# A drain between two users of one PSUM bank gives way to a one-column copy by ScalarE

## The chip, the cores and the metric

The kernel runs on one core of a Trainium2 chip. A core has five engines with a queue of their own: TensorE (PE in the profile, with its weight loads shown apart as PEld), VectorE (DVE), ScalarE (ACT), GpSimd (POOL) and SyncE (SP), which here only issues transfers. Every queue runs in the order in which it was filled, and engines wait for each other through semaphores. PE writes its products to PSUM, which has eight banks of 512 float32 columns on 128 partitions. The metric is the device time of one launch in microseconds.

## The reference, cut to what matters

The reference is a small latent diffusion trunk: two layers over 1024 latent tokens and 256 context tokens of width 1024, in float32. Layer 0 mixes tokens by differential attention, layer 1 by a state-space scan; each is followed by a squared-ReLU MLP. The change touches only the attention of layer 0:

```python
def attend(q, k, v):
    s = jnp.einsum('bqhcd,bkhcd->bhcqk', q, k).astype(jnp.float32)
    p = jax.nn.softmax(s, axis=-1)
    w = p[:, :, 0] - lam * p[:, :, 1]
    o = jnp.einsum('bhqk,bkhe->bqhe', w.astype(v.dtype), v)
    return rmsnorm(o, subln_g) * (1.0 - lambda_init)
```

There are eight heads. Each has two sets of queries and keys of width 64 (the index c), and one set of values of width 128. Latent queries read all 1280 keys, context queries the 256 context keys alone.

## The kernel before, in words

Float32 matmuls are made of three faster ones: every operand is split into a high and a low part, and high·high, high·low and low·high are added up in PSUM (`mm3`, L130 to L134; `split`, L136, whose high part is a copy by ACT at L137 and whose low part is a subtraction at L138).

**Attention (`phase_b`, L623)** goes through 72 units, nine for each head h. Unit u = 0 takes the 256 context queries, and each of the units u = 1 to 8 takes 128 latent queries. The profile shows them between about 224 and 903 us. In a unit the following happens:

- `scores` (L507) puts the scores of both sets into PSUM: set c = 0 in columns 0 to 1279, c = 1 in columns 1280 to 2559. The two sets use different halves of PE's rows (partitions 0 to 63 and 64 to 127), so a matmul of one set and a matmul of the other run at the same time. For u > 0 there are 21 matmuls in three groups of three rounds each: first c = 0 into bank 2 beside c = 1 into bank 3; then c = 0 into bank 0 beside c = 1 into bank 4; last c = 0 into bank 1 beside two short ones of c = 1, into banks 3 and 2. Bank 2 thus has two users: c = 0 in the first group, c = 1 in the third. Line 524 puts a drain of PE between the first and the second group.
- `maxima` (L529): DVE copies the scores of each set from PSUM to SBUF and takes their extremum on the way (L539).
- `exps` (L541): ACT takes exponentials and their sums (L549). `combine` (L552) makes p0 − lambda·p1 on DVE (L557 to L560).
- The transposes of the unit before (`w_part`, L562) and the copies that bring them to SBUF as high and low parts (`w_evac`, L577: L580 and L585 by ACT, L581 by DVE, L586 and L587 by POOL).
- Every second unit, the product with the values (`values`, L654) for a pair of units, and its copy out (`pair_out`, L665).
- Projections of the queries and keys of the next head (`proj_group`, L441), between the transposes.
- In five units out of nine, from head 1 on, `norm_pair` (L696) scales a pair of outputs of an older head: DVE multiplies (L697), ACT copies the high part (L137, tile `W<-W`), POOL subtracts the low part, and SP stores both. It is the last thing that such a unit gives to ACT. The condition in the loop (`n - 6 >= 9 and (n - 6) % 9 < 5`) makes it happen in the units u = 6, 7, 8 and in u = 0, 1 of the next head.

The order on PE, DVE, ACT and POOL in this phase is the order in which the loop is written (`manual`, L589); SP's transfers are placed by the scheduler. Dependencies are kept by the framework: two users of one PSUM bank are ordered by a semaphore whenever they are on different engines, and need none when both are on PE. After this phase the scheduler sets the order of all engines.

Of the kernel before, what the change touches and what calls it, by code (L numbers as in the profile page):

```python
# [9 lines left out]
AF = mybir.ActivationFunctionType  # L10
# [37 lines left out]
def shaped(ap, dims):  # L48
    if len(dims) == 1:
        return ap  # L50
    names = "abcd"[: len(dims)]
    kw = {n: d for n, d in zip(names[1:], dims[1:])}
    return ap.rearrange(f"p ({' '.join(names)}) -> p {' '.join(names)}", **kw)
# [17 lines left out]
class Prog:  # L71
# [410 lines left out]
    def lam_setup(self):  # L482
        nc, I = self.nc, self.I
        t, pr = self.fv(0, 256), self.fv(1, 2, 64)
        self.dma(t, I["attn_lambda"].rearrange("o a b -> o (a b)").to_broadcast((128, 256)))
        t4 = shaped(t, (2, 2, 64))
        nc.vector.tensor_tensor(pr, t4[:, :, 0], t4[:, :, 1], ALU.mult)
        st = self.lamc = self.cst.tile([128, 12], F32, name="lamc")
        nc.vector.tensor_reduce(st[:, 0:2], pr, AX.X, ALU.add)
        nc.scalar.activation(st[:, 2:4], st[:, 0:2], AF.Exp)  # L490
        nc.scalar.activation(st[:, 4:6], st[:, 2:4], AF.Ln)
        nc.vector.tensor_tensor(st[:, 4:6], st[:, 0:2], st[:, 4:6], ALU.subtract)
        nc.vector.tensor_scalar(st[:, 4:6], st[:, 4:6], 1.0, None, ALU.add)
        nc.vector.tensor_tensor(st[:, 2:4], st[:, 2:4], st[:, 4:6], ALU.mult)
        nc.vector.tensor_tensor(st[:, 6:7], st[:, 3:4], st[:, 2:3], ALU.subtract)
        nc.vector.tensor_scalar(st[:, 6:7], st[:, 6:7], -0.2, None, ALU.add)
        self.neglam = st[:, 6:7]
        self.dma(st[:, 7:8], I["attn_subln"].rearrange("o e -> e o"))
        nc.vector.tensor_scalar(st[:, 7:8], st[:, 7:8], 0.8, None, ALU.mult)
        self.sg = st[:, 7:8]  # L500
        self.ones = st[:, 8:9]
        nc.vector.memset(self.ones, 1.0)


# [2 lines left out]
    def scores(self, u, Q, K):  # L507
        mm = self.nc.tensor.matmul

        def tiles(qs, *parts):  # L510
            for n, (i, j) in enumerate(self.TERMS):
                for c, k0, k1, o in parts:
                    rows = slice(64 * c, 64 * c + 64)
                    mm(self.PS[:, o : o + k1 - k0], Q[rows, i, qs], K[j][rows, k0:k1], start=n == 0, stop=n == 2)  # L514

        if u == 0:
            for t in range(2):
                tiles(slice(128 * t, 128 * t + 128), (0, 0, 256, 512 * t), (1, 0, 256, 1024 + 512 * t))
            return
        qs = slice(128 * ((u - 1) % 2), 128 * ((u - 1) % 2) + 128)  # L520
        part = lambda c, k0, k1: (c, k0, k1, 1280 * c + k0)
        tiles(qs, part(0, 1024, 1280), part(1, 256, 512))

        self.nc.tensor.drain()
        tiles(qs, part(0, 0, 512), part(1, 768, 1280))
        tiles(qs, part(0, 512, 1024), part(1, 512, 768), part(1, 0, 256))

# [1690 lines left out]
```

## Time and profile before

| | |
|---|---|
| median of 3 runs | 2986.89 us (2981.88 to 2988.55) |
| the profiled execution's own time | 2989.72 us |
| its span, first to last instruction | 2987.9 us |
| mean granted clock of PE | 0.977 |
| the phase with the changed line, 223.8 to 903.0 us | 679.2 us |
| busy in it: PE, DVE, ACT, POOL | 615.85, 509.44, 372.11, 414.68 us |
| one head of it, 487.6 to 570.3 us | 82.7 us |

The last three lines come from the view that gives the busy time of each engine in a stretch. Rows of the timeline give the start in us, the duration in us, the engine, the line, the operation with its tiles and how many instructions are merged; in square brackets stands how long the engine was idle before it and which instruction ended that. Ends of matmuls are modelled. The head from 487.6 to 570.3 us, which the prediction follows, is head 3 counting from 0.

### The profile page before, as it was taken

To read this page: it belongs to the slowest core of one execution; us is meant where nothing else is said; L and a number is where in the kernel's file an instruction comes from. 1 tells how busy PE (TensorE), PEld (TensorE's weight loads), DVE (VectorE), ACT (ScalarE), POOL (GpSimd) and SP (SyncE) were. 2 spreads that over 40 slices of the span, in tenths; PEclk is the share of its full clock that TensorE was granted. 3 is DMA by queue.
4 is the path that set the end of the run, shared out by engine and by line. 5 is a ranking of instruction groups with operands and counts; after the bars stand their busy time and mean duration, and the time that the engine had idled before them with its cause. 6 is when DMAs were issued, how large, how long until landed. Compare 5 with 4: busy or idle time off the path is not lost.

```text
span 2987.9 us, 44389 instructions
## 1 busy us (share of the span) xinstructions
PE 2802.8 (94%) x16048; PEld 2323.3 (78%) x16048; DVE 1944.3 (65%) x2782; ACT 1314.9 (44%) x2406; POOL 1071.6 (36%) x923
## 2 busy tenths in 40 slices
PE   6998999999899999999999999788899899999999
PEld 4686878878777787788777778578788678888887
DVE  5356787777764554444478774789734687758566
ACT  3424555555553753333422231367534643334443
POOL 2313566666653600000100001689501443337323
PEclk9999999999999999999999999889999999999999
DMA  9953444444635546422566674568934244457544
GB/s 267 299 193 132 126 152 145 154 143 135 206 119 157 148 140 189 128 95 84 190 177 186 183 232 115 155 174 263 290 124 151 82 141 159 152 193 273 167 136 141
DMA packets 415240, 500.36 MB, mean 167 GB/s; under 512 B 56630, under 2 KB 291372, under 8 KB 413868
## 3 DMA queue, kind: packets, MB, share of 16 engines
q1 hardware_dynamic: 415020, 497.53, 53.6%
q8 instruction: 126, 2.06, 0.3%
q14 instruction: 94, 0.77, 0.1%
HBM read 342.90 MB, written 150.31 MB: 165 GB/s over the span
## 4 chain that ended last, share of the span: by engine, by line
PE 38%; DVE 4%; DMA 3%; issue 2%; POOL 2%; ACT 1%; SPq 0%; DVEq 0%; POOLq 0%; ACTq 0%
PE PS L132 11%; PE PS L134 11%; PE PS L133 11%; PE PS L1704 2%; PE PS L1739 1%; DMA K<-in_mlp_w 1%; DVE FD L1722 1%; DVE FD L1619 1%; DMA W<-Ad 1%; DVE FD L1713 1%; DVE H L138 1%; PE PS L1156 0%; DMA H<-xa 0%; PE PS L1736 0%; POOL FD L1608 0%
## 5 line engine op out<-in xcount | busy, mean ns | idle before, releaser
L132 PE MATMUL PS<-H,R 128*128 128x512 f32 (+1 forms) x840 | 312.9, 378 | 23.3 <-ACT F L585 15.9
L133 PE MATMUL PS<-H,R 128*128 128x512 f32 (+1 forms) x840 | 308.3, 367 | 5.2 <-POOL H L138 5.2
L132 PE MATMUL PS<-H 128*128 128x512 f32 x776 | 303.1, 392 | 4.4 <-ACT H L137 4.4
L134 PE MATMUL PS<-H,R 128*128 128x512 f32 (+1 forms) x840 | 307.2, 367 | 0.0
L133 PE MATMUL PS<-H 128*128 128x512 f32 x776 | 303.6, 391 | 0.0
L134 PE MATMUL PS<-H 128*128 128x512 f32 x776 | 302.0, 390 | 0.8 <-DVE H L138 0.8
L137 ACT ACTIVATE R<-W 128x512 fp32r<-128x512 f32 (+1 forms) x191 | 136.1, 717 | 197.6 <-PE PS L133 139.1
L549 ACT ACTIVATE F<-F,stat 128x1280 f32<-128x1280 f32 x128 | 174.4, 1362 | 96.0 <-DVE F L539 95.8
L132 PE MATMUL PS<-R,H 128*128 128x512 f32 x532 | 213.5, 404 | 1.5 <-ACT R L137 1.4
L133 PE MATMUL PS<-R,H 128*128 128x512 f32 x532 | 208.9, 393 | 0.0
L134 PE MATMUL PS<-R,H 128*128 128x512 f32 x532 | 207.3, 393 | 1.2 <-DVE H L138 1.2
L138 DVE TENSOR_TENSOR H<-W,H 128x512 fp32r<-128x512 f32 (+1 forms) x146 | 141.9, 981 | 101.2 <-ACT H L137 98.7
L138 DVE TENSOR_TENSOR R<-W,R 128x512 fp32r<-128x512 f32 (+1 forms) x154 | 141.7, 926 | 96.8 <-ACT R L137 78.8
L132 PEld LDWEIGHTS PS<-H,R 128*128 128x128 f32 x840 | 163.5, 195 | 49.3 <-ACT F L585 17.3
L539 DVE TENSOR_SCALAR_CACHE_REDUCE F<-PS 128x1280 f32<-128x1280 f32 x128 | 185.2, 1483 | 23.8 <-PE PS L514 23.8
L586 POOL TENSOR_SCALAR R<-F 128x256 fp32r<-128x256 f32 (+1 forms) x128 | 128.7, 1006 | 178.7 <-ACT F L585 156.6
L137 ACT ACTIVATE H<-W 128x512 fp32r<-128x512 f32 (+2 forms) x167 | 107.7, 653 | 184.5 <-PE PS L133 118.8
L133 PEld LDWEIGHTS PS<-H,R 128*128 128x128 f32 x840 | 164.5, 196 | 28.7 <-POOL H L138 6.8
L134 PEld LDWEIGHTS PS<-H,R 128*128 128x128 f32 x840 | 164.0, 195 | 25.7 <-issue 1.2
L132 PEld LDWEIGHTS PS<-H 128*128 128x128 f32 x776 | 145.9, 188 | 37.3 <-ACT H L137 5.3
L514 PE MATMUL PS<-R,R 64*128 64x256 f32 (+1 forms) x1380 | 157.2, 348 | 15.4 <-DVE F L539 6.7
L134 PEld LDWEIGHTS PS<-H 128*128 128x128 f32 x776 | 145.8, 188 | 31.8 <-DVE H L138 1.2
(439 smaller groups left out, 7295.9 us busy)
## 6 DMA issues: line engine op xcount, KB each, us to landing
W<-in_mlp_w SPq DMA_DIRECT2D x184, 256.0 KB
Ad<-F SPq DMA_DIRECT2D x112, 256.0 KB
W<-Ad SPq DMA_DIRECT2D x112, 256.0 KB
W<-in_ada_w SPq DMA_DIRECT2D x32, 512.0 KB
W<-in_mlp_w SPq DMA_DIRECT2D x32, 512.0 KB
H<-hidd SPq DMA_DIRECT2D x64, 256.0 KB
U<-in_ada_w SPq DMA_DIRECT2D x32, 512.0 KB
W<-in_s_w_glu SPq DMA_DIRECT2D x64, 256.0 KB
```

What stands on the lines that cost most here:

```text
L132: mm(out, ah, bh, start=first, stop=False, **kw)
L133: mm(out, ah, bl, start=False, stop=False, **kw)
L134: mm(out, al, bh, start=False, stop=last, **kw)
L137: self.nc.scalar.activation(hi, src, AF.Copy)
L138: (lo_eng or self.nc.vector).tensor_tensor(lo, src, hi.bitcast(F32), ALU.subtract)
L514: mm(self.PS[:, o : o + k1 - k0], Q[rows, i, qs], K[j][rows, k0:k1], start=n == 0, stop=n == 2)
L539: ts(p[c], self.PS[:, 1280 * c : 1280 * c + 1280], 1.0, None, ALU.mult, ALU.min, accum_out=sm[:, c : c + 1])
L549: nc.scalar.activation(p[c], p[c], AF.Exp, bias=sm[:, c : c + 1], scale=-1.0, accum_out=sn[:, 0:1] if c else s0[:, u + 1 : u + 2])
L586: nc.gpsimd.tensor_scalar(hi, t, 1.0, 0.0, ALU.mult, ALU.add)
L1619: v.scalar_tensor_tensor(y, w, r, x, ALU.mult, ALU.add)
L1704: mm(b[:, o : o + 160], X[:, d, i, 64 * j : 64 * j + 128], U[:, 4 * n + i, cols], start=True, stop=True)
L1713: v.tensor_tensor(four(t), x, four(P), ALU.mult)
```

## The change

The drain is taken out. In its place ACT copies one column of bank 2, the first of those that the first group of matmuls fills, to a spare column of a small tile (`seen`, in the tile `lamc`). The copy reads a bank that PE has written and will write again, so it waits for the first group, and the matmul of the third group that writes bank 2 waits for the copy.

```diff
-        self.ones = st[:, 8:9]
+        self.ones, self.seen = st[:, 8:9], st[:, 10:11]
         nc.vector.memset(self.ones, 1.0)
...
         tiles(qs, part(0, 1024, 1280), part(1, 256, 512))
-
-        self.nc.tensor.drain()
+        self.nc.scalar.activation(self.seen, self.PS[:, 1024:1025], AF.Copy)
         tiles(qs, part(0, 0, 512), part(1, 768, 1280))
         tiles(qs, part(0, 512, 1024), part(1, 512, 768), part(1, 0, 256))
```

Lines behind the copy have a number lower by one in the changed kernel: L549 becomes L548, and so on. The copy itself is L523.

**ACT's queue** in head 3, from the splits at the end of unit 0 to the first copy-out of transposes in unit 2; `W<-W` is the high part in `norm_pair`, `FC<-PS 128x256` the copy of `pair_out`, `lamc<-PS` the new copy. Before:

```order
L464 ACTIVATE FC<-PS 128x512 [waits DMAHW2_49,DMAHW1_49,DMAHW7_49,DMAHW0_49,PE_49]
L137 ACTIVATE R_105<-W 128x512 [waits DMAHW2_49]
L137 ACTIVATE W<-W 128x256 [waits DMAHW5_49,DVE_49,Pool_49]
L549 ACTIVATE F_1812,FC<-F_1812,stat 128x1280 [waits DVE_49]
L549 ACTIVATE F_1812,stat<-F_1812,stat 128x1280 [waits DVE_49,Activation_49]
L580 ACTIVATE R_105<-PS 128x512 [waits PE_49]
L665 ACTIVATE FC<-PS 128x256 [waits DMAHW3_49]
L137 ACTIVATE W<-W 128x256 [waits DMAHW0_49,DVE_49,Pool_49]
L580 ACTIVATE R_105<-PS 128x4x128 [waits PE_49,Activation_49]
```

And in the changed kernel:

```order
L464 ACTIVATE FC<-PS 128x512 [waits DMAHW2_49,DMAHW1_49,DMAHW7_49,DMAHW0_49,PE_49]
L137 ACTIVATE R_105<-W 128x512 [waits DMAHW2_49]
L137 ACTIVATE W<-W 128x256 [waits DMAHW5_49,DVE_49,Pool_49]
L523 ACTIVATE lamc<-PS 128x1 [waits PE_49]
L548 ACTIVATE F_1812,FC<-F_1812,stat 128x1280 [waits DVE_49]
L548 ACTIVATE F_1812,stat<-F_1812,stat 128x1280 [waits DVE_49,Activation_49]
L579 ACTIVATE R_105<-PS 128x512 [waits PE_49]
L664 ACTIVATE FC<-PS 128x256 [waits DMAHW3_49]
L137 ACTIVATE W<-W 128x256 [waits DMAHW0_49,DVE_49,Pool_49]
L523 ACTIVATE lamc<-PS 128x1 [waits PE_49,Activation_49]
L579 ACTIVATE R_105<-PS 128x4x128 [waits PE_49,Activation_49]
```

Each copy stands behind everything that the unit before gave to ACT, and here the last of that is the split of `norm_pair`.

**PE's queue** at the scores of unit 2 of head 3. Before (the drain stands between the first six and the seven of 512 columns, and isn't listed):

```order
L514 MATMUL PS<-R_1811,R_105 128x256 [waits DVE_49]
L514 MATMUL PS<-R_1811,R_105 128x256 x5
L514 MATMUL PS<-R_1811,R_105 128x512 x7
L514 MATMUL PS<-R_1811,R_105 128x256 x2
L514 MATMUL PS<-R_1811,R_105 128x512
L132 MATMUL PS<-R_105 128x256 [waits Activation_49]
```

And in the changed kernel:

```order
L514 MATMUL PS<-R_1811,R_105 128x256 [waits DVE_49]
L514 MATMUL PS<-R_1811,R_105 128x256 x5
L514 MATMUL PS<-R_1811,R_105 128x512 x7
L514 MATMUL PS<-R_1811,R_105 128x256
L514 MATMUL PS<-R_1811,R_105 128x256 [waits Activation_49]
L514 MATMUL PS<-R_1811,R_105 128x512
L132 MATMUL PS<-R_105 128x256
```

The 15th of the 21 matmuls now waits for ACT, and six more of the scores stand behind it, then everything else that PE does.

**SP's queue** in the same unit, as a difference; `R<-Qd` loads the queries of the next pair of units, `on<-W` stores what `norm_pair` made, and `W<-od` loads what the next one takes:

```order
-L80 DMA R_105<-Qd 128x2x256
-L80 DMA on<-W 128x256 x2
-L80 DMA W<-od 128x256
+L80 DMA on<-W 128x256 x2
+L80 DMA W<-od 128x256
+L80 DMA R_105<-Qd 128x2x256
```

The load of the queries goes behind the stores and the load of `norm_pair`. On DVE the first `maxima` of each unit waits for ACT as well as for PE. After the attention phase the scheduler has exchanged some neighbours on all engines, without adding or removing any.

## The prediction, made before the run

> **What bounds the kernel now.** I read the page's busy times and chain first, then the busy times in the attention phase, then who waits for whom there.
>
> ```profile
> PE 2802.8 (94%) x16048; PEld 2323.3 (78%) x16048; DVE 1944.3 (65%) x2782; ACT 1314.9 (44%) x2406; POOL 1071.6 (36%) x923
> PE 38%; DVE 4%; DMA 3%; issue 2%; POOL 2%; ACT 1%; SPq 0%; DVEq 0%; POOLq 0%; ACTq 0%
> ```
> ```profile
> 487.60:570.30 82.70, 76.91 (x556) 66.26 (x555) 65.78 (x102) 47.23 (x95) 54.29 (x52) 0.98 0.47 146
> ```
> ```profile
> ACT F L549 <- DVE F L539: 95.8, 60, 4.5
> PEld PS L514 <- issue: 36.3, 113, 3.4
> ```
>
> PE is busy 94% of the span and leads the chain. In one head of the attention it works 76.91 of 82.70 us, so it has 5.8 us of slack a head, and a stall beyond that lengthens the head. ACT is busy 47.23 us, but its queue often stands: the exponentials wait for the maxima (95.8 us in all). The 36.3 us before score matmuls that only "issue" explains hold the drains.
>
> **What the drain costs.** It has no price of its own in the trace; its records measure how long it lay in the queue:
>
> ```profile
> L524 PEldq DRAIN  x64: 632/2050/3457, 241.7 to 890.0; - x64
> ```
> ```profile
> 487.60 0.62 PE L514 MATMUL PS<-R,R 64*128 64x256 f32 x6
> 488.31 1.19 PE L514 MATMUL PS<-R,R 64*128 64x512 f32 x8
> 489.91 0.39 PE L132 MATMUL PS<-R 128*128 128x256 f32 x1
> 505.44 2.38 PE L514 MATMUL PS<-R,R 64*128 64x256 f32 x21
> ```
> ```profile
> 488.30 1.47 PEld L514 LDWEIGHTS PS<-R,R 64*128 64x128 f32 x15 [0.29 <-issue]
> ```
> ```profile
> 507.85 1.49 DVE L539 TENSOR_SCALAR_CACHE_REDUCE F<-PS 128x1280 f32<-128x1280 f32 x1 [0.58 <-PE PS L514]
> ```
>
> After the first six matmuls the weight loads stand still for 0.29 us: that is the drain. The issue time gives an upper bound, 36.3/64 = 0.57 us a unit, which still holds the entry into the scores; I take 0.3 us, nearest to the row of the gap itself. All 64 units together are then worth 19 us at most (36 by the upper bound), and only where PE sets the end. The Trainium skill ("TensorE: Matmul & The Clock Gate", section "Step-by-step: what each phase is for") lets the array's drain hide under the next matmul's fill and prices an exposed one at about 175 ns; by that the 64 would be worth an estimated 11 us instead of 19.
>
> The same rows place the new wait. The eight matmuls from 488.31 are those that start before 489.2, so the 15th, which will wait, starts 1.6 us after the scores do, and 1.3 us without the drain. From it to PE's next work are 0.7 us (489.91), and to the maxima 0.8 us (505.44 + 1.6 + 0.8 = 507.85, where DVE was waiting for the scores).
>
> **What the copy costs.** The nearest rows are ACT's smallest copies from PSUM; the copy's neighbour in the queue is the split of `norm_pair`:
>
> ```profile
> L673 ACT ACTIVATE FC<-PS x40: 162/166/172, 268.6 to 921.4; 128x2 f32<-128x2 f32 x40
> ```
> ```profile
> L137 ACT ACTIVATE W<-W x30: 416/418/420, 374.4 to 833.2; 128x256 fp32r<-128x256 f32 x30
> ```
>
> With the handover I take 0.2 us from the end of the ACT instruction ahead to the 15th matmul. The bounds are 0.1 (ACT starts the next one before the last ends) and 0.4 (the 256-column split). ACT has room for 64 such copies (13 us over the phase); what decides is when its queue gets to them. So the 15th matmul starts at the later of two times: 1.3 us after the scores began, or 0.2 us after ACT has finished everything that the unit before gave it. The 30 splits of `norm_pair` come in six repetitions of five; one in five precedes a unit 0, which has no copy, so 24 copies have one ahead of them. I follow head 3; "shift" is how much later something happens than today.
>
> Units 1 and 2:
>
> ```profile
> 490.59 0.42 ACT L137 ACTIVATE W<-W 128x256 fp32r<-128x256 f32 x1 [1.76 <-POOL R L138]
> ...
> 498.99 0.42 ACT L137 ACTIVATE W<-W 128x256 fp32r<-128x256 f32 x1 [3.36 <-POOL FC L470]
> ```
> ```profile
> 488.95 1.56 DVE L697 SCALAR_TENSOR_TENSOR W<-W,lamc 128x256 f32<-128x256 f32 x1
> 490.43 1.48 DVE L539 TENSOR_SCALAR_CACHE_REDUCE F<-PS 128x1280 f32<-128x1280 f32 x1
> ...
> 497.43 1.48 DVE L697 SCALAR_TENSOR_TENSOR W<-W,lamc 128x256 f32<-128x256 f32 x1
> 498.83 1.48 DVE L539 TENSOR_SCALAR_CACHE_REDUCE F<-PS 128x1280 f32<-128x1280 f32 x1
> ```
> ```profile
> 494.13 2.38 PE L514 MATMUL PS<-R,R 64*128 64x256 f32 x21
> ...
> 497.57 0.38 PE L133 MATMUL PS<-R 128*128 128x256 f32 x1 [0.74 <-DVE R L581]
> ...
> 498.27 0.60 PE L572 MATMUL PS<-ident,F 128*128 128x128 f32 x4
> ```
>
> Today DVE goes from the multiplication of `norm_pair` (L697) straight to the maxima, whose scores have long been there. With the copy, L697 must end, then ACT's split, then the copy, then the rest of the scores. Unit 1: ACT is done at 491.0, the 15th matmul starts at 491.2 instead of 489.2, and PE goes on at 491.9: shift 2.0. The maxima start at 492.0: shift 1.6. In unit 2 the exponentials, the combine, L697 and the split follow the maxima, so ACT is done at 499.4 + 1.6 = 501.0. PE, having begun at 496.1, would be at the 15th at 497.4 and stands until 501.2. It resumes its next work at 501.9; the 0.74 us for which it waits today is swallowed, and the transposes after it start at 502.75: shift 4.5. The maxima start at 502.0: shift 3.2.
>
> Units 3 to 8:
>
> ```profile
> 506.04 0.62 ACT L137 ACTIVATE R<-W 128x512 fp32r<-128x512 f32 x1
> ...
> 512.89 0.39 ACT L459 ACTIVATE R<-PS 128x256 fp32r<-128x256 f32 x1
> ```
> ```profile
> 522.08 0.65 ACT L137 ACTIVATE R<-FC 128x512 fp32r<-128x512 f32 x1
> ```
> ```profile
> 541.00 0.42 ACT L137 ACTIVATE W<-W 128x256 fp32r<-128x256 f32 x1 [1.40 <-DVE W L697]
> ...
> 552.13 0.42 ACT L137 ACTIVATE W<-W 128x256 fp32r<-128x256 f32 x1 [3.41 <-POOL R L587]
> ```
> ```profile
> 523.38 0.66 PE L572 MATMUL PS<-ident,F 128*128 128x128 f32 x4 [1.47 <-DVE R L581]
> 537.93 2.37 PE L514 MATMUL PS<-R,R 64*128 64x256 f32 x21
> 540.26 0.66 PE L572 MATMUL PS<-ident,F 128*128 128x128 f32 x4
> ```
> ```profile
> 547.49 2.38 PE L514 MATMUL PS<-R,R 64*128 64x256 f32 x21
> 557.65 0.38 PE L132 MATMUL PS<-H,R 128*128 128x256 f32 x1 [2.90 <-ACT F L585]
> ```
> ```profile
> 540.89 1.48 DVE L539 TENSOR_SCALAR_CACHE_REDUCE F<-PS 128x1280 f32<-128x1280 f32 x1
> ...
> 551.97 1.48 DVE L539 TENSOR_SCALAR_CACHE_REDUCE F<-PS 128x1280 f32<-128x1280 f32 x1
> ```
>
> In unit 3 ACT is free about when PE arrives (506.66 against 506.7), in unit 4 before it: nothing is late, the drain's 0.3 is partly won, and DVE takes over PE's shift, about 4.4. In unit 5 ACT ends at 522.7 + 4.4 = 527.1; the 15th starts at 527.3, PE goes on at 528.0, where it waits today anyway (1.47 for DVE): shift 4.6. Unit 6 wins 0.3. In unit 7 ACT ends at 541.4 + 4.4, the 15th starts at 546.0, PE goes on at 546.7: shift 6.4; the maxima at 546.8: shift 5.9. In unit 8 ACT ends at 552.55 + 5.9, the 15th starts at 558.65: PE shift 9.5, maxima at 559.45, shift 7.5. Then PE's 2.90 us for ACT swallows the difference: ACT's work follows the maxima, and everything goes on with **7.5 us a head**. Bounds: if only the four passes through split, copy and rest of the scores counted (0.42 + 0.2 + 0.8 = 1.4 each), 5.7; if PE's five stalls of 2.3, 3.8, 2.3, 2.5 and 3.4 all added up, 14.3.
>
> SP's moved load of queries, now behind stores that follow the split, leaves at about 503, and unit 3 needs it at 509.9; it costs nothing, and would stall PE if it took over 6 us. The copy holds nothing back on ACT, since what is behind it waits for the same scores.
>
> **The clock.**
>
> ```profile
> 558.30:561.70 3.40, 3.40 (x18) 3.40 (x17) 1.19 (x3) 0.42 (x1) 3.23 (x5) 0.50 0.99 336
> 523.40:526.80 3.40, 3.40 (x18) 2.87 (x19) 3.40 (x4) 1.61 (x2) 3.32 (x5) 1.00 0.43 164
> ```
>
> After PE's wait of 2.90 us the granted clock was 0.50 for 3.4 us, after the one of 1.47 it stayed at 1.00. Half speed for 3.4 us loses 1.7 us of matmuls. The long stall of unit 8 takes the place of the 2.90 us; that of unit 2 is new, and PE leads behind it: **1.7 us a head**. The others lie between 2.3 and 2.5 us and stay open: 0 to 1.7 each. The Trainium skill (the same page, section "What's actually happening") halves the clock only after an idle window of about 3.4 us; by that the short stalls would cost nothing, and even unit 2's not always. The trace has it already after 2.90 us.
>
> **The sum.** Six repetitions × (7.5 + 1.7) = 55 us. The 16 units outside them win up to 0.3 each, of which I count half: −2. So the profiled execution's 2989.72 us become 3043, and as it lies 2.8 us above the median of its runs, 3040 us. By the bounds: 6 × 5.7 − 5 = +29 gives 3016; 6 × 14.3 + 6 × 1.7 = +96 gives 3083.
>
> **The rivals.**
> *The drain's time is won, the copy is on time* (faster): for it speaks that ACT is less than half busy and that in units such as 4 it is free first. Then 64 × 0.3 = 19 us, 2968. It decides if ACT reaches the copy within 1.3 us of the start of the scores; against it stand the four `W<-W` rows, which end 3.4, 5.3, 3.5 and 5.1 us after it.
> *The stalls only replace waits* (no change): PE idles 5.8 us a head anyway, 0.74 + 1.47 + 2.90 of it in the rows above. But these are already swallowed in the 7.5. If the splits came some 1.5 us earlier in the queue, the rest would be nothing: 2987.
> *The clock falls at every stall*: 1.7 us more in units 5 and 7 and as much again where the stalls last two such stretches, about 4 us more a head: 3064.
> *Milder*: the lengthened pass through L697 finds slack that I missed, half of the 7.5 stays and the clock doesn't fall: 3010.
>
> **How the numbers follow.** Chances: forecast 0.60, clock 0.15, milder 0.12, no change 0.05, won 0.08. The range runs from 3007 to 3072, which takes in the milder case and most of the clock's and leaves out the last two. A measurement of this kernel tells about 0.2%, 6 us, from no change. Faster 0.08, the same 0.05, slower 0.87.
>
> **What would show it.** Right: score matmuls that wait for ACT's `lamc<-PS` in units 1, 2, 5, 7 and 8, by 2 to 4 us each and some 80 us in all; heads of 91 to 93 us instead of 82.7; the drain's gap gone. Wrong in the mechanism: those waits under 20 us in all, or the copies running ahead of the splits. Wrong in size: waits as long as said, with heads that grow by under 4 us.

## The result, and the profile after

The changed kernel takes **3028.71 us** (median of 4 runs, 3025.62 to 3030.04), against 2986.88 us before on the same chip: ratio **1.0137** (95% interval 1.0122 to 1.0152), or 42 us more. Its profiled execution took 3030.04 us with a span of 3028.1 us, against 2987.9 us before. Nearly all of it lies in the attention phase, here in the busy times by stretch (length; busy time and count of PE, PEld, DVE, ACT and POOL; granted clock; DMA share and GB/s). After, then before:

```profile
223.80:944.00 720.20, 631.09 (x4357) 534.63 (x4356) 496.23 (x797) 379.88 (x805) 392.38 (x397) 0.93 0.43 136
587.00:676.00 89.00, 79.84 (x558) 67.98 (x557) 63.24 (x102) 48.20 (x103) 50.22 (x52) 0.94 0.43 135
```
```profile
223.80:903.00 679.20, 615.85 (x4362) 526.02 (x4361) 509.44 (x797) 372.11 (x741) 414.68 (x397) 0.96 0.46 145
570.30:653.00 82.70, 76.89 (x556) 66.19 (x555) 65.25 (x102) 47.25 (x95) 54.28 (x52) 0.98 0.47 146
```

The phase grew from 679.2 to 720.2 us, and the same head (head 4) from 82.7 to 89.0 us. Half of the 6.3 us of the head is PE being idle for longer (5.8 to 9.2 us), half is PE being busy for longer (76.9 to 79.8 us) with the same work, at a mean clock of 0.94 instead of 0.98.

Who waits for whom in the phase, after (total us, times, longest):

```profile
PEld PS L514 <- ACT lamc L523: 76.5, 46, 6.1
DVE F L538 <- PE PS L514: 64.5, 44, 4.2
PE PS L514 <- ACT lamc L523: 59.0, 33, 5.4
PEld PS L514 <- issue: 16.9, 43, 3.6
```

The first and third lines are the new wait: score matmuls stand 59.0 us for the copy, their weight loads 76.5 us. The drains' line ("issue", 36.3 us before) has fallen to 16.9. DVE waits 64.5 us for its scores, where it waited 23.8 before:

```profile
DVE F L539 <- PE PS L514: 23.8, 21, 4.4
```

The copy itself is small:

```profile
L523 ACT ACTIVATE lamc<-PS x64: 149/163/190, 244.7 to 934.7; 128x1 f32<-128x1 f32 x64
```

So is the wait its place in the queue? Units 1 and 2 of head 4, on PE, ACT and DVE:

```profile
587.01 1.55 PE L514 MATMUL PS<-R,R 64*128 64x256 f32 x14
590.50 0.86 PE L514 MATMUL PS<-R,R 64*128 64x256 f32 x7 [1.93 <-ACT lamc L523]
591.29 0.38 PE L132 MATMUL PS<-R 128*128 128x256 f32 x1
...
597.02 1.54 PE L514 MATMUL PS<-R,R 64*128 64x256 f32 x14
599.59 0.84 PE L514 MATMUL PS<-R,R 64*128 64x256 f32 x7 [1.03 <-ACT lamc L523]
```
```profile
589.98 0.42 ACT L137 ACTIVATE W<-W 128x256 fp32r<-128x256 f32 x1 [1.73 <-POOL R L138]
590.30 0.15 ACT L523 ACTIVATE lamc<-PS 128x1 f32<-128x1 f32 x1
...
599.06 0.42 ACT L137 ACTIVATE W<-W 128x256 fp32r<-128x256 f32 x1 [1.06 <-POOL adat L665]
599.39 0.15 ACT L523 ACTIVATE lamc<-PS 128x1 f32<-128x1 f32 x1
```
```profile
588.36 1.53 DVE L696 SCALAR_TENSOR_TENSOR W<-W,lamc 128x256 f32<-128x256 f32 x1
591.49 1.49 DVE L538 TENSOR_SCALAR_CACHE_REDUCE F<-PS 128x1280 f32<-128x1280 f32 x1 [1.60 <-PE PS L514]
...
598.50 0.48 DVE L696 SCALAR_TENSOR_TENSOR W<-W,lamc 128x256 f32<-128x256 f32 x1
```

ACT sits idle for 1.73 us with the copy behind it, because the split of `norm_pair` ahead of the copy isn't ready; the 15th matmul starts 0.10 us after the split has ended. In unit 2 the multiplication on DVE takes 0.48 us, where unit 1 of the same head needs 1.53 and where the prediction's row of before had 1.48. That will matter below.

And the clock, in stretches behind the waits of units 1, 5 and 7 of head 4:

```profile
592.00:595.40 3.40, 3.40 (x19) 3.40 (x18) 2.40 (x4) 2.36 (x3) 0.00 (x0) 0.50 0.46 123
626.20:629.60 3.40, 3.40 (x13) 2.79 (x12) 3.40 (x4) 1.55 (x2) 3.32 (x5) 0.50 0.45 165
646.60:650.00 3.40, 3.40 (x11) 2.88 (x11) 3.17 (x5) 2.04 (x3) 3.40 (x4) 0.51 0.20 68
```

Three stretches of half speed in this head, where the same head of before had one, behind the wait ahead of unit 0.

### The profile page after: what moved, and what is told of

Read it like the earlier page. It is cut to its first block, busy times and chain, and to the rows that moved or that the text cites. A ratio compares the mean times of both kernels' runs of the same rounds, so it can differ in the third digit from the quotient of the medians.

```text
span 3028.1 us, 44493 instructions
## 1 busy us (share of the span) xinstructions
PE 2821.8 (93%) x16048; PEld 2334.9 (77%) x16048; DVE 1925.1 (64%) x2782; ACT 1322.2 (44%) x2470; POOL 1041.8 (34%) x923
## 3 DMA queue, kind: packets, MB, share of 16 engines
q8 instruction: 126, 2.06, 0.3%
## 4 chain that ended last, share of the span: by engine, by line
PE 37%; DVE 4%; DMA 4%; issue 2%; POOL 2%; ACT 1%; SPq 0%; DVEq 0%; POOLq 0%; ACTq 0%
PE PS L132 11%; PE PS L134 11%; PE PS L133 11%; PE PS L1703 1%; PE PS L1738 1%; DVE H L138 1%; DVE FD L1618 1%; DMA W<-in_mlp_w 1%; DVE R L138 1%; PE PS L1155 0%; DMA K<-in_mlp_w 0%; DVE FD L1712 0%; DMA H<-xb 0%; PE PS L1161 0%; DMA ptd<-FD 0%
## 5 line engine op out<-in xcount | busy, mean ns | idle before, releaser
L538 DVE TENSOR_SCALAR_CACHE_REDUCE F<-PS 128x1280 f32<-128x1280 f32 x128 | 185.6, 1487 | 65.0 <-PE PS L514 64.5
L548 ACT ACTIVATE F<-F,stat 128x1280 f32<-128x1280 f32 x128 | 174.4, 1363 | 105.3 <-DVE F L538 105.1
L585 POOL TENSOR_SCALAR R<-F 128x256 fp32r<-128x256 f32 (+1 forms) x128 | 118.4, 925 | 232.8 <-ACT F L584 188.7
L514 PEld LDWEIGHTS PS<-R,R 64*128 64x128 f32 x1380 | 115.5, 189 | 106.3 <-ACT lamc L523 76.5
L132 PEld LDWEIGHTS PS<-H 128*128 128x128 f32 x776 | 146.6, 189 | 37.1 <-ACT H L137 5.0
```

What stands on the lines that cost most here:

```text
L132: mm(out, ah, bh, start=first, stop=False, **kw)
L538: ts(p[c], self.PS[:, 1280 * c : 1280 * c + 1280], 1.0, None, ALU.mult, ALU.min, accum_out=sm[:, c : c + 1])
L548: nc.scalar.activation(p[c], p[c], AF.Exp, bias=sm[:, c : c + 1], scale=-1.0, accum_out=sn[:, 0:1] if c else s0[:, u + 1 : u + 2])
L585: nc.gpsimd.tensor_scalar(hi, t, 1.0, 0.0, ALU.mult, ALU.add)
```

## The experiments

The theory to be tested: the copy costs what it does because it is queued behind the split of `norm_pair`; the size of the loss comes partly from the clock. Each ratio is against before, run on the same chip.

**The copy ahead of the split.** `norm_pair` of a unit is held back until the next unit has issued its scores, and the loads for the next `norm_pair` go behind it. DVE still multiplies ahead of its maxima, ACT gets the copy first.

```diff
+                    while held:
+                        norm_pair(*held.pop())
...
-                    norm_pair((n - 6) // 9 - 1, (n - 6) % 9)
+                    held.append(((n - 6) // 9 - 1, (n - 6) % 9))
```

> The copy stays and the drain stays out, but the split of norm_pair comes after the copy on ACT: norm_pair is given out between the scores and the maxima of the next unit, so its place on DVE is the same. My theory (the copy is late because it stands behind that split): the waits of the 15th score matmul in units 1, 2, 7 and 8 fall from 2.1, 1.2, 2.3 and 1.2 us to 0.3 us or less, only unit 5 (behind the split of the stored keys) still waits 2.2 us and costs about 1.5 us in each of six heads, so about 9 us of the 42 stay: 2990 to 3000 us. Rival (the order through ACT costs by itself, wherever the copy stands in the queue): the waits stay and it is 3015 us or more. Rival (the drain was worth far more than 0.3 us a unit): under 2975 us.

Measured: 2997.40 us, ratio 1.0043 (1.0028 to 1.0059). In its waits and in ACT's queue:

```profile
PEld PS L514 <- ACT lamc L523: 34.1, 45, 2.5
```
```profile
568.78 0.16 ACT L523 ACTIVATE lamc<-PS 128x1 f32<-128x1 f32 x1
570.64 0.42 ACT L137 ACTIVATE W<-W 128x256 fp32r<-128x256 f32 x1 [1.70 <-POOL R L138]
```

The same copy and the same split, 28 us apart in time by their order alone (0.94% of 2984 us; the move by itself, the control further down, can't be told from before). This settles the main question: two thirds of the loss are the place in the queue. In unit 5 the weight loads still wait up to 2.5 us, since there another split (the keys' `R<-FC`) stands ahead. The profiled execution of this kernel was the shortest of its runs, so it doesn't show where the rest of its median goes.

**The copy needed later.** The nine matmuls of the third group in another order, so that the first that needs the copy comes 18th, not 15th.

```diff
-        tiles(qs, part(0, 512, 1024), part(1, 512, 768), part(1, 0, 256))
+        late = ((0, 512, 1024), (1, 512, 768), (1, 0, 256))
+        for x, n in ((0, 0), (1, 0), (1, 1), (0, 1), (1, 2), (2, 0), (0, 2), (2, 1), (2, 2)):
```

> The changed kernel with the last nine score matmuls in another order: the three that write bank 2 come 15th, 18th and 19th to 21st no longer, but as 18th, 20th and 21st, so that PE has three more matmuls to do before it waits. The same work. If only the length of the wait counts, each late unit gets about 0.35 us back, five units in six heads: 10 us, 3018 us. If the half-speed stretches of the clock that follow the waits of 2.3 to 2.5 us belong to the loss (three in a head, each up to 1.7 us of PE time), and the shorter waits of about 2 us no longer bring them, it is 2995 to 3005 us. If the late copy is not what costs the time: 3029 us, unchanged.

Measured: 3028.35 us, 1.0143 (1.0125 to 1.0162): nothing won. Both gains that were expected failed; the time is the one set down for a late copy that doesn't matter, which the first experiment rules out. Where the 0.3 us went, on PE in head 4:

```profile
588.30 0.63 PE L530 MATMUL PS<-R,R 64*128 64x512 f32 x5
590.64 0.62 PE L530 MATMUL PS<-R,R 64*128 64x256 f32 x4 [1.71 <-ACT lamc L523]
...
600.47 1.00 PE L530 MATMUL PS<-R,R 64*128 64x256 f32 x4 [3.28 <-ACT lamc L523]
```

Unit 1's wait is 0.2 us shorter; here the clock didn't fall behind it, PE came to unit 2 after 8.3 instead of 10.0 us, and waited 3.28 us there. The chain of ACT and DVE sets the time, and PE's early arrival only lengthens a wait.

**The drain doubled, and the drain beside the copy.** A second drain between the second and third group of the kernel before; and the changed kernel with its drain put back behind the copy.

```diff
         self.nc.tensor.drain()
         tiles(qs, part(0, 0, 512), part(1, 768, 1280))
+        self.nc.tensor.drain()
```

> The kernel before with a second drain in each of the 64 units, between the second and the third group of score matmuls, and nothing else: the price of a drain by itself. By the gap of 0.29 us seen behind the first one: up to 19 us slower, less where DVE or ACT sets the end, 2995 to 3006 us. If the drain is nearly free: 2987 to 2990 us. If it costs the 0.57 us a unit of the upper bound: about 3020 us.

> The changed kernel with the drain put back behind the copy. My theory (in a late unit the wait for the copy hides the drain, in the units 3, 4 and 6 it does not): about 0.3 us in three units of a head, 4 to 8 us more than the changed kernel, 3033 to 3037 us. Rival (the change won the drain's 19 us and lost 61 elsewhere): 3048 us. Rival (the drain costs nothing): 3029 us.

Measured: 2991.17 us, 1.0023 (1.0011 to 1.0036), and 3030.36 us, 1.0160 (1.0128 to 1.0192). With two drains, on PEld:

```profile
490.91 0.54 PEld L514 LDWEIGHTS PS<-R,R 64*128 64x128 f32 x6 [0.29 <-issue]
491.95 0.78 PEld L514 LDWEIGHTS PS<-R,R 64*128 64x128 f32 x9 [0.50 <-issue]
```

A second gap appears, and 64 of them cost 7 us, 0.11 us each: less than the gap shows, and less than the 2995 to 3006 us that I expected. In head 3 of this trace the units 1, 3, 4, 6 and 7 take some 0.35 us longer each, and units 2 and 5, where PE waits for DVE, as much less: part of the gap comes out of waits that PE has anyway. The second kernel can't be told from the change alone, nor from the 4 to 8 us more that were expected. A kernel with neither drain nor copy would have the two users of the bank unordered; it wasn't tried.

**The clock alone.** In the late units the second group's six matmuls are done three times, so that PE works through 1.4 us of its wait.

```diff
...
-        tiles(qs, part(0, 0, 512), part(1, 768, 1280))
+        for _ in range(3 if late else 1):
+            tiles(qs, part(0, 0, 512), part(1, 768, 1280))
```

> The changed kernel; in the units whose copy is late (1, 2, 5, 7, 8 of the steady heads) the six matmuls of the second group are done three times over, behind the copy's issue, so that TensorE works through some 1.4 us of its wait of 2.3 to 2.5 us; each repetition starts its sum anew, so nothing else changes. Theory (the clock's fall behind the waits of units 1, 5 and 7 is what makes them cost what they do): no half-speed stretch follows the waits of units 5 and 7, unit 5's interval falls from +2.1 us to about +0.5, head length from 89.0 to 85 to 86.5, in all 3005 to 3018 where the change has 3029. Rival (the late handover alone costs it, the clock follows but sets nothing): 3027 to 3032. Third: the added matmuls reach beyond the wait and PE loses them: over 3033.

Measured: 3020.30 us, 1.0118 (1.0099 to 1.0138). The head from 669.6 us, then the stretch from unit 3 of this head to unit 3 of the next, then units 1 and 2 of the first and DVE's multiplication ahead of unit 2:

```profile
669.60:758.30 88.70, 82.63 (x612) 70.46 (x612) 64.29 (x101) 47.19 (x102) 52.03 (x50) 0.98 0.43 136
693.53:781.83 88.30, 82.20 (x616) 69.78 (x615) 64.67 (x102) 47.86 (x103) 52.92 (x51) 1.00 0.43 136
```
```profile
669.61 2.92 PE L514 MATMUL PS<-R,R 64*128 64x256 f32 x26
673.14 0.85 PE L514 MATMUL PS<-R,R 64*128 64x256 f32 x7 [0.61 <-ACT lamc L523]
...
678.15 2.93 PE L514 MATMUL PS<-R,R 64*128 64x256 f32 x26
683.20 0.92 PE L514 MATMUL PS<-R,R 64*128 64x256 f32 x7 [2.12 <-ACT lamc L523]
```
```profile
681.13 1.45 DVE L698 SCALAR_TENSOR_TENSOR W<-W,lamc 128x256 f32<-128x256 f32 x1
```

The clock is at 0.98 again, with one stretch of half speed a head instead of three, and yet the head takes 88.7 us. Unit by unit it did what the theory said (unit 5's interval, from the start of its scores to the start of the next unit's and against before, fell from +2.06 to +0.5 us, unit 1's from +3.5 to +2.0, unit 7's from +3.7 to +2.1), but the time came back in unit 2 (+4.0 instead of 0) and ahead of unit 0. So my expectation of 85 to 86.5 us fell. The second row goes further: there the clock doesn't fall at all, and the stretch still takes 88.30 us, against 88.99 for the one before it (unit 2 is 1.6 us shorter without the fall behind it, and unit 0 is 0.9 us longer). In the steady heads the falls of the clock aren't what sets the length. What this doesn't give is the price of the clock by itself: PE came to unit 2 1.5 us earlier, and the multiplication ahead of it took 1.45 us again, where the change has 0.48. The 8 us that the median lies below the change's come, in the trace, from heads 1 and 2 and from the stretch from head 6 to head 7, and the two intervals overlap.

**What the copy costs as an instruction.** The drain kept, and the same copy on ACT from a constant column of SBUF, waited for by nobody.

```diff
         self.nc.tensor.drain()
+        self.nc.scalar.activation(self.seen, self.ones, AF.Copy)
```

> The kernel before, drain kept, with the same one-column copy on ACT at the same place, but from a constant column in SBUF: nothing waits for it and it waits for nothing. It prices the 64 ACT instructions themselves. Theory: ACT is under half busy and they cost nothing, 2 us at most (ratio 0.9993 to 1.001). Rival (they lengthen ACT's chain behind the maxima by 0.15 us a unit): +10 us, ratio 1.003.

Measured: 2985.67 us, 1.0001 (0.9990 to 1.0011). 64 more instructions on ACT cost nothing that can be measured.

**What the end of a unit issues, behind the scores too.** Two kernels moved all of it, the second with the later order as well. In both, a split of the projection then reads its buffer after the next block has written it, so that part of the keys and queries comes from another block; the instructions and their sizes are the same.

```diff
-                next_post()
+                if post:
+                    held.append(post.pop(0))
```

> As e1_copy_ahead, and what the end of a unit puts into the queues (the splits behind the stores, the loads of keys and values for the next head) also goes behind the next unit's scores, so that unit 5's copy has only its unit's own exponentials and evacuations ahead. Theory: unit 5's wait falls from 2.4 us to 1.7 or less, no half speed follows it, and the rest of the wait only stands where PE waits for DVE anyway (1.47 us); with the drain's gap gone in the other units this ends 3 to 10 us below before (ratio 0.9967 to 0.999). Rival: the split of unit 5 is then late for its own reader or the wait is set by the exponentials, and it ends as e1_copy_ahead did, ratio 1.002 to 1.006.

> e6_ends_behind with the nine matmuls of the third group in e2_late_order's order, so that the first one that needs the copy comes 18th instead of 15th, some 0.3 us later. Theory: the short waits that are left (0.2 to 0.7 us in units 1, 2, 7, 8) shrink by 0.2 to 0.35 each and 1 to 5 us are won on e6_ends_behind (ratio 0.996 to 0.999). Rival (as in e2_late_order: PE only comes earlier to the next thing that waits for ACT or DVE): equal to e6_ends_behind within 0.1%.

Measured: 3009.57 us, 1.0082 (1.0066 to 1.0097), and 3005.49 us, 1.0075 (1.0059 to 1.0091): slower than moving `norm_pair` alone, against both theories. The wait of unit 5's weight loads did fall to 1.9 us, but, in the first of the two, the intervals of units 2 and 3 grew by 0.7 and 0.5 us or more, and that of unit 8 by up to 1.2 us. The splits that were moved were probably wanted earlier; that wasn't taken apart. The last kernel moves only the one split of unit 5, which is safe:

```diff
-                next_post()
+                if u == 4 and post:
+                    held.append(post.pop(0))
+                else:
+                    next_post()
```

> e1_copy_ahead, and behind the scores of unit 5 also the one split that ACT has ahead of its copy there (the 0.65-us split of the keys that the end of unit 4 issues, with its store and the loads of the next head's values and keys). Unit 4 starts no block of the projection, so the buffer that the split reads isn't written before it. All 64 copies stay. Theory (the wait of unit 5 is ACT's queue, and its size decides whether the clock falls): the wait falls from 2.42 to about 1.9 us as in e6_ends_behind, costs 0.3 us where no half speed follows and 1.5 where it does; ratio 1.001 to 1.003 where e1_copy_ahead had 1.0043. Rival (the split wasn't what held the copy): gap and ratio as in e1_copy_ahead, 1.0035 or more. Second rival (later loads make the next head wait): over 1.005.

Measured: 2993.75 us, 1.0031 (1.0019 to 1.0043): a bit below the first kernel, with overlapping intervals, and just above the 1.001 to 1.003 of its theory. Its unit 5 is the clearest case of what the clock goes by. PE stands idle for 1.5 us there in every head (its weight loads wait 1.9 us); the interval to unit 6 grows by 0.27 us in heads 3 and 6 and by 1.84 to 1.88 us in heads 1, 2, 4 and 5. Heads 3 and 4, cut at multiples of 3.41 us from the clock's own changes:

```profile
519.17:522.58 3.41, 3.27 (x30) 2.52 (x28) 2.45 (x7) 3.12 (x5) 0.08 (x1) 1.00 0.05 14
522.58:525.99 3.41, 1.82 (x14) 1.54 (x15) 3.38 (x5) 2.12 (x7) 2.74 (x3) 1.00 0.11 38
525.99:529.41 3.42, 3.42 (x17) 2.79 (x16) 3.42 (x6) 2.30 (x5) 3.34 (x4) 1.00 0.40 153
...
604.50:607.90 3.40, 1.66 (x16) 1.17 (x13) 3.11 (x5) 2.29 (x8) 2.29 (x3) 1.00 0.11 39
607.90:611.30 3.40, 3.40 (x11) 2.63 (x10) 3.40 (x6) 2.05 (x3) 3.32 (x4) 0.51 0.43 157
```

In head 3 the wait lies across a border and PE is busy 1.82 us in the worse window, and full speed stays; in head 4 it lies inside one window with 1.66 us, and half speed follows.

**The copy only where it is on time.** First in units 3, 4 and 6 with the drain elsewhere; then the first experiment with the drain back in unit 5 alone; and, as its control, the moved `norm_pair` with drains everywhere.

```diff
-        self.nc.scalar.activation(self.seen, self.PS[:, 1024:1025], AF.Copy)
+        if u in (3, 4, 6):
+            self.nc.scalar.activation(self.seen, self.PS[:, 1024:1025], AF.Copy)
+        else:
+            self.nc.tensor.drain()
```

> The copy only in units 3, 4 and 6, where it was on time; the other units keep the drain. Theory (a copy on time wins the drain's gap, and PE's wins are kept where nothing waits behind them): up to 24 x 0.3 = 7 us less than before, ratio 0.9977; with the trace's -0.1, -0.3 and -0.35 us for these units 6 us, ratio 0.998. Rival: PE only comes earlier to its waits of 1.47 us (unit 5) and 2.90 us (ahead of unit 0), which grow by as much: ratio 0.9995 to 1.0005. No copy here has a split ahead of it, so no loss is expected; over 1.002 would mean that a copy costs more than its place in the queue.

> e1_copy_ahead (norm_pair issued behind the scores of the next unit), with the drain back in unit 5 alone, whose copy there still came 2.4 us late. Theory: unit 5's +2.07 us is gone, the waits of 0.2 to 0.7 us in units 1, 2, 7 and 8 remain and are about paid for by the drains saved: ratio 0.998 to 1.001. Rival: the ratio of 1.0043 of e1_copy_ahead came from the order of norm_pair itself and stays, 1.003 to 1.005; then e11_drain_moved shows the same.

> The kernel before with the drain everywhere, and only norm_pair and the loads behind it issued after the scores of the next unit as in e1_copy_ahead. It prices the move alone. Theory: VectorE's order is as before and the move costs nothing, ratio 0.999 to 1.001. Rival: the later loads or splits cost it, ratio 1.003 to 1.005, and the copies of e1_copy_ahead cost nothing.

Measured: 2982.77 us, 0.9990 (0.9978 to 1.0002); 2989.93 us, 1.0014 (1.0002 to 1.0026); 2987.39 us, 1.0008 (0.9996 to 1.0020). Unit 5 of the first kernel, on PE:

```profile
514.89 2.39 PE L514 MATMUL PS<-R,R 64*128 64x256 f32 x21
519.02 0.66 PE L574 MATMUL PS<-ident,F 128*128 128x128 f32 x4 [1.74 <-DVE R L583]
```

A copy on time does save PE 0.1, 0.3 and 0.35 us in units 3, 4 and 6, but unit 5's wait for DVE grew from 1.47 to 1.74 us and took most of the first two. The gain can't be told from none. Copies up to 0.7 us late cost nothing that can be measured beside the control; giving unit 5 its drain back took the ratio from 1.0043 to 1.0014, some 9 us.

## Why the prediction was right, and where its sizes were off

The direction, the mechanism and the range (3007 to 3072, forecast 3040) held. By its steps:

- *The 15th matmul starts 0.2 us after ACT's instruction ahead, PE goes on 0.7 us and DVE 0.8 us later.* Held, within 0.2 us: 0.1, 0.8 and 1.0 us in both units above. In unit 1 it started 3.49 us after the scores began (forecast 3.6), PE went on at 4.28 (4.3) and the maxima at 4.48 us (4.4).
- *Waits in units 1, 2, 5, 7, 8 and nowhere else in a steady head.* Held. By the prediction's measure (later than 1.3 us after the scores began) they are, in head 4, 2.2, 1.3, 2.3, 2.4 and 1.3 us; forecast 2.3, 3.8, 2.3, 2.5 and 3.4. The long ones, of units 2 and 8, were oversized, and these two fall short of the 2 to 4 us that were named as the sign of being right. The waits in all, forecast at some 80 us, are 76.5 on the weight loads.
- *Heads of 91 to 93 us.* Missed: 89.0. The forecast was 7.5 + 1.7 = 9.2 us a head, the trace has 6.25 (the same unit 1 of heads 3 to 6 is shifted by 10.44, 16.70, 22.95 and 28.08 us). From unit 3 of one head to unit 3 of the next, the six repetitions cost 10.0, 5.1, 6.3, 6.3, 5.1 and 8.6 us: the first, which holds head 2's unit 2 (below), and the last cost about the forecast, the four in between don't. That makes 41 of the 42 us.

How much later the maxima of each unit start against before, added in each unit:

| unit | forecast | the change, head 4 | PE kept busy, head 4 |
|---|---|---|---|
| 1 | 1.6 | 0.2 | 0.5 |
| 2 | 1.6 | 0.7 | 1.65 |
| 3 | 1.2 + 1.7 for the clock | 1.1 | 2.6 |
| 4 to 6 | 0 | 1.5 | 0 |
| 7 | 1.5 | 1.6 | 1.6 |
| 8 | 1.6 | 1.15 | 0 |
| sum | 9.2 | 6.25 | 6.35 |

The last column is the experiment in which only unit 2's wait is followed by half speed, as the forecast assumed. Units 2 to 7 there come within 0.3 us of it. In the change, units 3 to 6 together (2.6 us) come near the forecast's 2.9 by luck: the fall of the clock that was counted in unit 3 didn't come, and another one behind unit 5 did. What failed is named by rows 1 and 8, which differ in both columns, and by row 2 of the change:

- **The durations on DVE (units 8 and 2).** The forecast carried L697 along with its 1.48 and 1.42 us. In the changed kernel it takes 0.48 in unit 2 and 0.66 us in unit 8; with PE kept busy, the whole way from unit 7's maxima to it is 8.79 instead of 9.74 us. POOL's rows say why. Before, in units 2 and 8 of head 3, and after, in the same units of head 4:

```profile
497.35 1.28 POOL L470 TENSOR_TENSOR FC<-FC,W 128x512 f32<-128x512 f32 x1
...
550.47 1.29 POOL L587 TENSOR_TENSOR R<-F,R 128x512 fp32r<-128x512 f32 x1
```
```profile
598.08 0.61 POOL L665 TENSOR_TENSOR adat<-FC 128x256 f32<-128x256 f32 x1 [6.87 <-ACT FC L664]
...
655.59 1.60 POOL L586 TENSOR_TENSOR R<-F,R 128x512 fp32r<-128x512 f32 x1
```
```profile
656.81 0.66 DVE L696 SCALAR_TENSOR_TENSOR W<-W,lamc 128x256 f32<-128x256 f32 x1
```

The multiplication ends 0.28 us after the end of a POOL instruction that was running when it began: 498.63 and 498.91, 551.76 and 552.05, 598.69 and 598.98, 657.19 and 657.47; so in 23 of the 27 cases of before in which POOL was at work. The shortest take 0.48 us. Where it is longer, its duration is what is left of that instruction and 0.28 us, so it changes as soon as DVE and POOL are shifted against each other, as they were here. The Trainium skill ("SBUF — State Buffer", section "SBUF: two separate sides") has the rule: DVE with two SBUF inputs and POOL take turns at one pair of ports, and who comes second waits out the other's whole instruction; the trace agrees. Head 2 of the changed kernel is the counter-check: there L696 took 1.45 us in unit 2, and the wait came out at 3.75 us, the forecast's 3.8:

```profile
414.00 1.55 PE L514 MATMUL PS<-R,R 64*128 64x256 f32 x14
419.05 1.43 PE L514 MATMUL PS<-R,R 64*128 64x256 f32 x7 [3.51 <-ACT lamc L523]
```

- **The clock (units 1 and 3).** The forecast kept the half speed ahead of unit 0, with unit 8's long stall as its cause, and added one behind unit 2. With unit 8 waiting only 1.3 us, and PE 0.94 us for ACT behind it instead of 2.89, the one ahead of unit 0 was gone: that gave unit 1 back its 1.4. The fall behind unit 2 didn't come either, and those that "stay open", behind units 1, 5 and 7, all came. So 1.7 us net was forecast, and the falls were three instead of one, in other places.
- **What they add up to.** The rival in which every stall makes the clock fall was right about the falls of units 5 and 7 and wrong about the price: it added 4 us a head, and with PE kept busy the head is 0.3 us shorter without them, with the multiplication ahead of unit 2 longer by 1 us. As far as these runs show, PE's lost time and its waits replace each other while ACT's and DVE's chain sets the head.
- *The drain is worth 19 us at most, −2 counted.* Held in size: a second drain costs 7 us, and taking it out where the copy is on time can't be told from nothing. The prediction's other figure, an estimate of 11 us from the 175 ns that the Trainium skill ("TensorE: Matmul & The Clock Gate", section "Single matmul latency") states for the array to drain, is nearer to these 7 us than my 19.
- *Unit 5 costs 0.2 us, since PE waits there anyway.* Wrong by the clock: its interval grew by 2.06 us, with half speed behind the wait, and by 0.5 with PE kept busy.

## What to carry to other kernels

A wait handed to another engine costs what stands ahead of it in that engine's queue, not what the waiting instruction takes: here 0.16 us of copy, free by itself, cost 42 us behind splits that weren't ready, and 13 with unit 5's alone left behind one. Before adding an ordering through a second engine, look in the timeline for the idle time just ahead of the place where it will be queued. And when a change shifts DVE against POOL, the durations of before don't move along with the DVE instructions that overlap POOL's.

## What was not expected of the hardware

The clock's changes lie on a grid of 3.413 us, to within 0.005 us in each of the 14 profiled kernels. Counting PE's busy time in each window of the attention phase (340 to 950 us) that began at full clock, over all of them: with under 1.3 us idle, none of some 2050 was followed by half speed; with 1.3 to 2.0 us, 61 of 134; with 2.0 us or more, all 85. So a wait of PE under 1.3 us, with no other idle time near it, was safe, and one of 4 us can't be (it leaves 2.0 us in one window). Between them it mattered where the wait lay on the grid, as in heads 3 and 4 above. PE's idle time alone doesn't settle that band: the window of head 3 above has 1.6 us idle and kept full speed, while windows with 1.5 us idle lost it in the first kernel that moved all that a unit's end issues. What else counts stays open. That the window runs freely is also what the Trainium skill says ("TensorE: Matmul & The Clock Gate", section "What's actually happening"), and the trace agrees; it speaks of an idle window as the condition, and here a window with 2.0 of its 3.4 us idle was always enough and one with 1.4 us sometimes, so the measurement decides.
